# Exponents of the state space decay tables: put together by DMAs instead of by two matmuls in PSUM

## The chip, the cores and the metric

The kernel runs on one core of one Trainium2 chip. The metric is the device time of one execution in microseconds (us), lower is better. Three executions of the kernel before took 2723.22, 2725.10 and 2725.86 us; the median is 2725.1 us. A core has a matrix engine (PE, with its weight loads on a row of their own, PEld), a vector engine (DVE), an activation engine (ACT), GpSimd (POOL), and SyncE (SP), which here only issues DMAs. Each of them works through its own queue in order. Working tiles lie in SBUF; matmuls write to PSUM, which has 8 banks of 128 x 512 numbers.

## The reference, cut to what matters

The model is two blocks of two layers each, for one sequence of 512 positions and width 1024. The change touches one of its mixers, a bidirectional state space layer with 32 heads in 4 groups and chunks of 128 positions. The scan of one direction is, in short:

```python
def step(h, inp):                       # one chunk of 128 positions
    qq, kk, vv, aa = inp                # aa: log decay, <= 0
    cs = jnp.cumsum(aa, axis=1)         # running sum of the log decay
    seg = cs[:, :, None] - cs[:, None, :]
    decay = jnp.exp(jnp.where(mask, seg, -jnp.inf))   # 128 x 128 table of a head and chunk
    qk = jnp.einsum('bjgn,blgn->bjlg', qq, kk)
    y_intra = jnp.einsum('bjlgh,blghp->bjghp', qk[..., None] * decay, vv)
    y_inter = jnp.einsum('bjgn,bghnp->bjghp', qq, h) * jnp.exp(cs)[..., None]
    ...                                 # the state h of the next chunk
y = scan(q, k, v_f, a_f, include the diagonal) + flip(scan(flipped, a_b, without the diagonal))
```

So each head and each direction has a table of exp(running sum at j - running sum at l), cut off by a triangular mask. The kernel adds the tables of the two directions, multiplies by qk once for both, and multiplies the result into v.

## The kernel before, in words

All work is done on transposed activations, 8 tiles of 128 x 512. Matrices of weights come from HBM in pieces of 128 x 1024 (512 KB), each loaded by `wload` (L419 to L429): a DMA on SP's queue into one of 3 buffers `wr`, a rounded copy `wh` on ACT (L427), and the rest `wl` on DVE (L414), each with 3 buffers too. `mm3` (L431 to L435) multiplies one 128 x 128 block of such a piece in three matmuls of 128 x 512, so one piece feeds 24 matmuls.

The state space layer is `ssd`. Its decays are computed early by `dtev`: running sums by matmuls with triangular ones, the natural layout copied out as `c2` twice side by side, transposed (L1141), and split into a rounded half and a rest that lie in the upper and lower 64 partitions of `hl` (L1142, L1143). Then come four groups, each run by `scan(g)`; `weave` (L215) mixes into each scan pieces of the independent large matmuls: `xbc` and `zg` (projections of later groups) and `oproj` (output projection of earlier ones). In `scan(g)`: first states of the chunks (`state`, L1232) and what they contribute (`carry`, three matmuls and an add to `inter` on POOL, L417), and then, head by head, `decay(i)` and, for each pair of heads, `intra(pr)`.

`decay(i)` makes the table of head i for all four chunks, 128 x 512. For each of the two directions it takes a bank of PSUM and makes two matmuls: one with the broadcast selector column of the head, `sel`, on `hl`, which writes the row of running sums into all 128 partitions (L1274), and one with the identity on the mask (L1275), which adds 0 or -1e30. Four exponentials on ACT (L1278), one per chunk, read the bank, add the running sum of the own position as bias, and write SBUF. POOL adds the two directions (L1281), DVE multiplies by qk (L1282). `intra(pr)` multiplies two heads' tables into v in PSUM (L1292) and adds the `inter` tiles by matmuls with the identity (L1296).

SBUF working tiles come from a ring of 78 slots: `T()` takes the slot that was given back longest ago, `rel` gives one back. Nothing checks time there; an instruction that writes a slot waits for the last one that used it. The Tile layer then puts the instructions of the program into one order per engine by readiness, so the order on an engine is not that of the source.

## Time and profile before

The profiled execution took 2723.65 us, with a span of 2721.9 us between the first and the last instruction of the trace, 1.75 us less.

| | before |
|---|---|
| median of 3 executions | 2725.1 us |
| profiled execution, its span | 2723.65 us, 2721.9 us |
| PE busy | 2671.9 us, 98% |
| DVE, ACT, POOL busy | 62%, 45%, 13% |
| mean DMA traffic | 90 GB/s |

Busy time is what a view adds up; matmuls overlap in it, so the mean of one matmul there (some 390 ns) is longer than the time from one start to the next, which is read from the timeline. "Idle before" is the time for which an engine had nothing running before a group's instructions, with the instruction that ended it.

### The profile page before, as it was taken

What the parts mean: (1) busy time and instruction counts of PE and PEld (TensorE: products, weight loads), DVE (VectorE), ACT (ScalarE), POOL (GpSimd) and SP (SyncE); (2) the same over time, 40 slices, a digit from 0 to 9 for tenths busy, and PEclk for the clock granted to TensorE, in tenths of its full rate; (3) what the DMA queues carried; (4) which work ended last, traced back from release to release, by engine and by line L of the source; (5) the groups of instructions that cost most, each with busy time, mean ns of one, the idle gap of its engine ahead of it and who ended that gap; (6) DMA issues with size and microseconds to landing.
All of it is one profiled execution on the core that took longest, in us unless ns stands there. A gap on an engine that the chain in (4) does not pass through costs nothing. (4 is left out here: it accounts for less than half of the span.)

```text
span 2721.9 us, 34509 instructions
## 1 busy us (share of the span) xinstructions
PE 2671.9 (98%) x13136; PEld 2161.2 (79%) x13136; DVE 1674.4 (62%) x3029; ACT 1220.0 (45%) x2136; POOL 345.4 (13%) x416
## 2 busy tenths in 40 slices
PE   9999999999999899999999999999999999999999
PEld 7887888888877677888888877688888888888887
DVE  7765687733898687687762688644343467643442
ACT  5536454422576665554432368633133345432331
POOL 3101300001111211320000245210000100100000
PEclk9999999999999999999999999999999999999999
DMA  4223322243211121323243312223323222323232
GB/s 163 67 90 101 117 93 93 92 123 111 93 56 62 57 68 57 125 82 101 93 127 93 115 43 67 74 69 94 93 93 97 91 79 63 106 89 97 93 99 80
DMA packets 77206, 245.29 MB, mean 90 GB/s; under 512 B 8688, under 2 KB 10096, under 8 KB 77040
## 3 DMA queue, kind: packets, MB, share of 16 engines
q1 hardware_dynamic: 76896, 243.04, 28.3%
q8 instruction: 103, 1.69, 0.3%
q14 instruction: 63, 0.52, 0.1%
q10 hardware_dynamic: 144, 0.05, 0.0%
HBM read 232.57 MB, written 10.49 MB: 89 GB/s over the span
## 5 line engine op out<-in xcount | busy, mean ns | idle before, releaser
L433 PE MATMUL b<-v,wh 128*128 128x512 f32 (+1 forms) x2964 | 1155.5, 390 | 0.3 <-DVE v L1256 0.3
L434 PE MATMUL b<-v,wh 128*128 128x512 f32 (+1 forms) x2964 | 1145.3, 386 | 0.0
L435 PE MATMUL b<-v,wl 128*128 128x512 f32 (+1 forms) x2964 | 1145.0, 387 | 0.2 <-DVE wl L414 0.2
L427 ACT ACTIVATE wh<-wr 128x1024 fp32r<-128x1024 f32 (+3 forms) x401 | 411.4, 1027 | 856.8 <-PE b L434 732.2
L414 DVE TENSOR_TENSOR wl<-wr,wh 128x1024 fp32r<-128x1024 f32 (+3 forms) x401 | 478.0, 1193 | 485.9 <-ACT wh L427 484.0
L433 PEld LDWEIGHTS b<-v,wh 128*128 128x128 f32 x2964 | 557.3, 188 | 123.3 <-issue 3.5
L435 PEld LDWEIGHTS b<-v,wl 128*128 128x128 f32 x2964 | 556.6, 188 | 122.0 <-DVE wl L414 0.9
L434 PEld LDWEIGHTS b<-v,wh 128*128 128x128 f32 x2964 | 557.5, 188 | 120.7 <-issue 2.8
L417 POOL TENSOR_TENSOR v<-v,v 128x256 f32<-128x256 f32 (+1 forms) x146 | 173.5, 1190 | 1535.3 <-ACT v L607 1266.7
L406 ACT ACTIVATE v<-v 128x512 fp32r<-128x512 f32 x172 | 107.9, 630 | 222.8 <-DVE v L1071 101.2
L434 PE MATMUL b<-v,v 128*128 128x256 f32 (+6 forms) x536 | 167.6, 316 | 10.0 <-DVE v L410 8.1
L433 PE MATMUL b<-v,v 128*128 128x256 f32 (+6 forms) x536 | 172.6, 336 | 3.6 <-ACT v L409 2.9
L435 PE MATMUL b<-v,v 128*128 128x256 f32 (+6 forms) x536 | 163.9, 309 | 0.0
L407 DVE TENSOR_TENSOR v<-v,v 128x512 fp32r<-128x512 f32 x172 | 120.7, 706 | 68.8 <-ACT v L406 68.4
L434 PEld LDWEIGHTS b<-v,v 128*128 128x128 f32 (+2 forms) x536 | 101.4, 189 | 24.8 <-DVE v L410 13.3
L433 PEld LDWEIGHTS b<-v,v 128*128 128x128 f32 (+2 forms) x536 | 98.0, 189 | 21.8 <-issue 4.9
L435 PEld LDWEIGHTS b<-v,v 128*128 128x128 f32 (+2 forms) x536 | 101.3, 189 | 5.8 <-issue 0.7
L1060 DVE TENSOR_TENSOR v<-b,v 128x512 f32<-128x512 f32 x88 | 60.4, 690 | 72.4 <-PE b L435 70.6
L409 ACT ACTIVATE v<-v,prm 128x256 fp32r<-128x256 f32 (+1 forms) x112 | 66.4, 598 | 75.1 <-DVE v L265 51.1
L433 PE MATMUL b<-wh,v 128*128 128x512 f32 (+1 forms) x240 | 94.5, 394 | 1.4 <-DVE nv L502 1.1
L434 PE MATMUL b<-wl,v 128*128 128x512 f32 (+1 forms) x240 | 92.4, 385 | 1.0 <-DVE wl L414 1.0
L435 PE MATMUL b<-wh,v 128*128 128x512 f32 (+1 forms) x240 | 92.0, 385 | 0.6 <-DVE v L410 0.6
(372 smaller groups left out, 2706.8 us busy)
## 6 DMA issues: line engine op xcount, KB each, us to landing
wr<-in_w_f SPq DMA_DIRECT2D x128, 512.0 KB, 3.6
wr<-in_w_up SPq DMA_DIRECT2D x88, 512.0 KB, 3.4
wr<-in_w_dn SPq DMA_DIRECT2D x28, 448.0 KB, 3.3
wr<-in_w_xbc SPq DMA_DIRECT2D x24, 512.0 KB, 3.4
wr<-in_w_o SPq DMA_DIRECT2D x20, 512.0 KB, 3.5
wr<-in_w_dn SPq DMA_DIRECT2D x18, 512.0 KB, 3.5
wr<-in_w_z SPq DMA_DIRECT2D x16, 512.0 KB, 3.6
wr<-in_w_co SPq DMA_DIRECT2D x16, 512.0 KB, 3.4
```

Source lines behind the costliest of these rows:

```text
L406: nc.scalar.activation(hi, src, AF.Copy)
L407: nc.vector.tensor_sub(lo, src, hi.bitcast(F32))
L409: nc.scalar.activation(hi, src, AF.Copy, scale=scale)
L414: self.nc.vector.tensor_sub(out, x, y)
L417: self.nc.gpsimd.tensor_add(out, x, y)
L427: nc.scalar.activation(hi, raw, AF.Copy)
L433: mm(ps, lh, rh, start=start, stop=False)
L434: mm(ps, lh, rl, start=False, stop=False)
L435: mm(ps, ll, rh, start=False, stop=stop)
L1060: nc.vector.tensor_mul(h, ps, rb)
```

## The change

The masks leave SBUF: instead of two 128 x 128 tiles in bf16, an input `mdec` in HBM holds both, repeated for the four chunks, as 2 x 128 x 512 numbers. `dtev` copies and transposes the running sums once, not twice side by side, copies them to a tile and writes them to HBM as `csd` (64 rows of 512). For each head and direction a tile of SBUF is then filled in two steps: `masks(i)` loads the mask from HBM by a DMA on SP's queue (256 KB), and `rows(i)` adds the head's row of running sums to all 128 partitions by an accumulating DMA on POOL's queue, whose source is one row of 2 KB of `csd`, broadcast. `masks` is called three heads ahead, `rows` two. The exponentials read that tile and write it in place. The 128 matmuls, their 64 banks and `hl` go.

```diff
-        hl = self.R()
+        csd = self.dp.tile([64, S], F32, name="csd")
...
             for c in range(4):
-                nc.tensor.transpose(b[:, c * P:(c + 1) * P], c2[:, c].rearrange("p a b -> p (a b)"), self.c("id"))
-            nc.scalar.activation(hl, b, AF.Copy)
-            nc.vector.tensor_sub(hl[64:128, :], b[64:128, :], hl[64:128, :].bitcast(F32))
+                nc.tensor.transpose(b[0:64, c * P:(c + 1) * P], c2[:, c], self.c("id"))
+            csT = self.T()
+            nc.scalar.activation(csT[0:64], b[0:64], AF.Copy)
             self.brel(b)
+            nc.sync.dma_start(out=csd, in_=csT[0:64])
+            self.rel(csT)
...
+            def masks(i):
+                if i < 8:
+                    Ex[i] = [self.T(4, P) for _ in range(2)]
+                    for d in range(2):
+                        nc.sync.dma_start(out=Ex[i][d], in_=self.a["mdec"][d])
+
+            def rows(i):
+                if i < 8:
+                    for d in range(2):
+                        r = 32 * d + 8 * g + i
+                        nc.gpsimd.dma_start(out=Ex[i][d].rearrange("p a b -> p (a b)"),
+                                            in_=csd[r:r + 1, :].to_broadcast([P, S]), accum_op=ALU.add)
 
             def decay(i):
+                masks(i + 3)
+                rows(i + 2)
                 h = 8 * g + i
-                t = [None, None]
-                for d, m in ((0, self.mupb), (1, self.mlowb)):
-                    b = self.bank()
+                t = Ex.pop(i)
+                for d in range(2):
                     r = 32 * d + h
-                    nc.tensor.matmul(b, self.sel[:, r:r + 1].to_broadcast([P, P]), hl, start=True, stop=False)
-                    nc.tensor.matmul(b, self.idb, m.unsqueeze(1).to_broadcast([P, 4, P]), start=False, stop=True)
-                    t[d] = self.T(4, P)
                     for c in range(4):
-                        nc.scalar.activation(t[d][:, c], b[:, c * P:(c + 1) * P], AF.Exp,
-                                             bias=nat["sl"][:, c, r:r + 1])
-                    self.brel(b)
+                        nc.scalar.activation(t[d][:, c], t[d][:, c], AF.Exp, bias=nat["sl"][:, c, r:r + 1])
                 nc.gpsimd.tensor_add(t[0], t[0], t[1])
...
             weigh(1, 0)
+            for i in range(3):
+                masks(i)
...
             self.rel(B)
+            for i in range(2):
+                rows(i)
             decay(0)
```

Line numbers of the changed kernel differ from those of before by a few: `mm3` is L430 to L432 there, the mask's DMA L1270, the row's DMA L1277, the exponentials L1288, POOL's add L1289, `intra` L1300 and L1304.

On PE, in the first scan, the matmuls of the first tables stood between the `carry` matmuls (L433 to L435 on `v`) before:

```order
L435 MATMUL b_6959<-v_6884,v_6688 128x512
L1274 MATMUL b_6967<-v_6346,sel 128x512 [waits PE_49]
L1275 LDWEIGHTS idb
L1275 MATMUL b_6967<-mupb,idb 128x512
L1274 MATMUL b_6975<-v_6346,sel 128x512
L1275 LDWEIGHTS idb
L1275 MATMUL b_6975<-mlowb,idb 128x512
L433 MATMUL b_6985<-v_6899,v_6687 128x512 [waits PE_49,Activation_49]
```

In the changed kernel, at the same place, the first matmul of `intra` (L1300) has moved up among the projections (`wh`) and the last `carry`:

```order
L432 MATMUL b_6995<-v_6907,v_6684 128x512
L430 MATMUL b_7007<-v_5954,wh_7009 128x512 [waits PE_49]
L431 MATMUL b_7007<-v_5955,wh_7009 128x512
L430 MATMUL b_7094<-v_5954,wh_7096 128x512
L431 MATMUL b_7094<-v_5955,wh_7096 128x512
L1300 MATMUL b_7145<-v_6759,v_6692 64x128 [waits DMASW1_49,DVE_49]
L430 MATMUL b_7180<-v_5954,wh_7182 128x512 [waits DVE_49,Activation_49]
L431 MATMUL b_7180<-v_5955,wh_7182 128x512
```

What moved: the matmuls of the tables are gone, and nearly all the others keep their order; the first multiplication with a finished table comes earlier, before the last `carry`.

On SP, in the second scan, the weight loads (`wr`) followed each other before:

```order
L426 DMA wr_7777<-in_w_xbc 128x1024 [waits DMAHW7_49,DVE_49]
L426 DMA wr_7834<-in_w_xbc 128x1024 [waits DMAHW0_49,DVE_49]
L426 DMA wr_7928<-in_w_xbc 128x1024 [waits DMAHW1_49,DVE_49,Activation_49]
L426 DMA wr_8016<-in_w_co 128x1024 [waits DMAHW2_49,DVE_49]
L426 DMA wr_8108<-in_w_co 128x1024 [waits DMAHW3_49,DVE_49]
```

In the changed kernel masks stand between them, each with a wait for the last user of its slot (DVE, PE, POOL or ACT):

```order
L423 DMA wr_7996<-in_w_co 128x1024 [waits DMAHW1_49,DVE_49]
L1270 DMA v_7752<-in_mdec 128x512 [waits DVE_49,DMAHW5_49,PE_49,Activation_49]
L1270 DMA v_7725<-in_mdec 128x512 [waits DMAHW6_49,PE_49]
L1270 DMA v_7898<-in_mdec 128x512 [waits DMAHW7_49,PE_49]
L1270 DMA v_7807<-in_mdec 128x512 [waits DMAHW0_49,Pool_49]
L1270 DMA v_7753<-in_mdec 128x512 [waits DMASW2_49,DVE_49]
L1270 DMA v_7808<-in_mdec 128x512 [waits DMAHW2_49]
L1270 DMA v_7724<-in_mdec 128x512 [waits DMAHW3_49,DVE_49]
L423 DMA wr_8072<-in_w_co 128x1024 [waits DMAHW4_49,DVE_49]
L1270 DMA v_7862<-in_mdec 128x512 [waits DMAHW5_49,DVE_49]
L1270 DMA v_7897<-in_mdec 128x512 [waits DMAHW6_49,Pool_49]
L423 DMA wr_8108<-in_w_co 128x1024 [waits DMAHW7_49,DVE_49,Activation_49]
```

What moved: seven masks now stand ahead of one weight load and two more ahead of the next, and one mask of each lot waits for POOL.

On POOL, in the second scan, the two adds of `inter` (L417) were followed by the adds of the tables before:

```order
L417 TENSOR_TENSOR v_7670<-v_7668,v_7653 128x512 [waits DVE_49,Activation_49]
L417 TENSOR_TENSOR v_7726<-v_7724,v_7597 128x512 [waits DVE_49]
L1281 TENSOR_TENSOR v_7731<-v_7731,v_7739 128x512 [waits Activation_49]
L1281 TENSOR_TENSOR v_7761<-v_7761,v_7769 128x512 [waits DMAHW0_49,Activation_49]
L1281 TENSOR_TENSOR v_7818<-v_7818,v_7826 128x512 [waits PE_49,Activation_49]
```

In the changed kernel the rows' DMAs stand around them, each with a wait for its mask (a DMAHW semaphore):

```order
L1277 DMA v_7752<-csd 128x512 [waits DVE_49,DMAHW5_49,PE_49,Activation_49]
L1277 DMA v_7725<-csd 128x512 [waits DMAHW6_49,PE_49]
L414 TENSOR_TENSOR v_7662<-v_7660,v_7645 128x512 [waits DVE_49]
L1277 DMA v_7898<-csd 128x512 [waits DMAHW7_49,PE_49]
L1277 DMA v_7807<-csd 128x512 [waits DMAHW0_49,Pool_49]
L1277 DMA v_7753<-csd 128x512 [waits DMAHW1_49,DVE_49]
L1277 DMA v_7808<-csd 128x512 [waits DMAHW2_49]
L1277 DMA v_7724<-csd 128x512 [waits DMAHW3_49,DVE_49]
L414 TENSOR_TENSOR v_7718<-v_7716,v_7589 128x512 [waits DVE_49]
L1289 TENSOR_TENSOR v_7752<-v_7752,v_7753 128x512 [waits DMASW6_49,DMASW2_49,Activation_49]
```

What moved: seven DMAs now stand ahead of the second `inter` add, and each waits for its mask. The tables of this scan's first three heads are not among these rows: their DMAs and adds stand earlier, in the first scan.

On ACT the 256 exponentials are spread over more places between the SiLU functions of `xbc` and `zg`: its queue holds 45 table loads around them (21 at L1288, 15 at L1163, 9 at L1175) where the kernel before has 31 (13 at L1278, 13 at L1165, 4 at L1177, 1 at L1130).

## Rows read from the trace of the kernel before

**Rows 1.** The page's busy time, share of the span and instructions of each engine.
```profile
PE 2671.9 (98%) x13136; PEld 2161.2 (79%) x13136; DVE 1674.4 (62%) x3029; ACT 1220.0 (45%) x2136; POOL 345.4 (13%) x416
```

**Rows 2.** Windows: stretch, length, busy time by engine, granted clock, DMA share, GB/s.
```profile
690.00:790.00 100.00, 98.55 (x496) 80.69 (x497) 87.20 (x158) 59.12 (x87) 8.38 (x11) 0.98 0.24 80
790.00:1110.00 320.00, 304.02 (x1541) 227.98 (x1540) 244.66 (x337) 205.13 (x434) 72.43 (x50) 0.99 0.19 61
...
796.00:846.00 50.00, 44.96 (x252) 32.58 (x252) 40.13 (x47) 39.32 (x85) 15.94 (x11) 1.00 0.23 74
846.00:870.00 24.00, 23.56 (x108) 19.01 (x109) 22.02 (x42) 11.22 (x15) 0.39 (x1) 1.00 0.10 28
870.00:923.00 53.00, 48.20 (x248) 35.49 (x246) 40.33 (x49) 41.53 (x92) 15.61 (x10) 1.00 0.14 48
...
920.00:930.00 10.00, 3.84 (x13) 2.31 (x14) 6.32 (x6) 7.57 (x17) 3.76 (x3) 0.67 0.11 35
```

**Rows 3.** Waits of PE from 690 to 1120 us: total, times, longest.
```profile
PE b L1292 <- DVE v L1282: 10.4, 4, 4.6
PE b L434 <- DVE v L410: 2.3, 4, 1.2
```

**Rows 4.** Timeline of PE around one head's four matmuls: start, duration, instruction.
```profile
819.34 0.39 PE L435 MATMUL b<-v,wl 128*128 128x512 f32 x1
819.56 0.40 PE L1274 MATMUL b<-v,sel 128*128 128x512 f32 x1
819.80 0.39 PE L1275 MATMUL b<-mupb,idb 128*128 128x512 bf16 x1
819.84 0.58 PE L1274 MATMUL b<-v,sel 128*128 128x512 f32 x1
820.26 0.39 PE L1275 MATMUL b<-mlowb,idb 128*128 128x512 bf16 x1
```

**Rows 5.** Line L1274 and line L1141: duration min/median/max, first and last start.
```profile
L1274 PE MATMUL b<-v,sel x64: 390/578/585, 790.4 to 1106.0; 128*128 128x512 f32 x64
...
L1141 PE MATMUL b<-cst,v x4: 270/272/272, 756.5 to 756.8; 128*128 128x128 f32 x4
```

**Rows 6.** Groups by line on ACT: count, busy us, mean ns, idle before.
```profile
L1278 ACT ACTIVATE v<-b,v 128x128 f32<-128x128 f32 x256 | 69.5, 414 | 4.1 <-PE b L1275 4.0
L427 ACT ACTIVATE wh<-wr 128x1024 fp32r<-128x1024 f32 x47 | 49.5, 1060 | 56.8 <-PE b L434 41.9 <-issue 14.9
L1278 ACT ACT_TABLE_LOAD x13 | 16.7, 1283 | 0.2
...
L1853 ACT ACTIVATE v<-v,gta 128x128 f32<-128x128 f32 x16 | 5.8, 389 | 0.0
```

**Rows 7.** Groups by line on DVE and POOL.
```profile
L414 DVE TENSOR_TENSOR wl<-wr,wh 128x1024 fp32r<-128x1024 f32 x48 | 59.0, 1234 | 15.6 <-ACT wh L427 15.6
L1282 DVE TENSOR_TENSOR v<-v,v 128x512 f32<-128x512 f32 x32 | 29.9, 936 | 27.0 <-POOL v L1281 27.0
...
L1281 POOL TENSOR_TENSOR v<-v,v 128x512 f32<-128x512 f32 x32 | 45.7, 1430 | 96.5 <-ACT v L1278 87.0 <-issue 4.9 <-DVE v L1158 4.5
```

**Rows 8.** DMA issues: KB each, median us from issue to landing.
```profile
wr<-in_w_xbc SPq DMA_DIRECT2D x22, 512.0 KB, 3.4
v<-xs SPq DMA_DIRECT2D x7, 256.0 KB, 2.9
...
outT<-v SPq DMA_DIRECT2D x2, 128.0 KB, 1.7
```

**Rows 9.** Waits of SP's queue from 690 to 1120 us, and its issue, min/median/max ns.
```profile
SPq L426 <- DVE wl L414: 374.8, 44, 34.0
...
L619 SPq DMA_DIRECT2D xf<-v x16: 319/320/432, 318.4 to 1185.2; - x16
```

**Rows 10.** Timeline of PE after its longest wait in the scans.
```profile
923.26 0.61 PE L1292 MATMUL b<-v,v 128*64 128x128 f32 x2 [4.57 <-DVE v L1282]
926.77 1.12 PE L1292 MATMUL b<-v,v 128*64 128x128 f32 x6 [2.90 <-DVE v L1282]
...
928.83 0.63 PE L433 MATMUL b<-v,wh 128*128 128x512 f32 x1
929.26 0.63 PE L434 MATMUL b<-v,wh 128*128 128x512 f32 x1
```

More of the change, by code (lines that the diff above doesn't have):

```diff
@@ L92, in _constants @@
     ramp = ramp.reshape(P, 768)
-    return {"cst": cst, "cs0": cs0.astype(f), "ramp": ramp.astype(f)}
+    mdec = np.stack([np.tile(np.where(p <= c, 0.0, NEG), (1, 4)), np.tile(np.where(p > c, 0.0, NEG), (1, 4))])
+    return {"cst": cst, "cs0": cs0.astype(f), "ramp": ramp.astype(f), "mdec": mdec.astype(f)}
 def _rpb_index():
@@ L324, in __init__ @@
         self.mlab = self.cp.tile([P, P], BF16, name="mlab")
-        self.mupb = self.cp.tile([P, P], BF16, name="mupb")
-        self.mlowb = self.cp.tile([P, P], BF16, name="mlowb")
         self.sel = self.cp.tile([P, 64], F32R, name="sel")
@@ L334, in consts @@
         nc.vector.tensor_copy(self.mlab, self.c("mmla"))
-        nc.vector.tensor_copy(self.mupb, self.c("mup"))
-        nc.vector.tensor_copy(self.mlowb, self.c("mlow"))
         nc.vector.tensor_add(self.sel, self.c("id")[:, 0:64], self.c("id")[:, 64:128])
@@ L1125, in dtev @@
                 nc.tensor.matmul(tot[:, c, :], self.ones, la[:, c, :], start=True, stop=True)
-            c2 = self.T(4, 2, 64)
-            for j in range(2):
-                nc.vector.tensor_copy(c2[:, :, j, :], cs)
+            c2 = self.T(4, 64)
+            nc.vector.tensor_copy(c2, cs)
             nc.scalar.activation(nat["dec"], tot, AF.Exp)
-            nc.scalar.activation(nat["ecs"], c2[:, :, 0, :], AF.Exp)
-            nc.vector.tensor_sub(la, tot, c2[:, :, 0, :])
+            nc.scalar.activation(nat["ecs"], c2, AF.Exp)
+            nc.vector.tensor_sub(la, tot, c2)
             self.brel(b)
@@ L1136, in dtev @@
             nc.scalar.activation(v, v, AF.Ln)
-            nc.vector.tensor_sub(nat["sl"], v.rearrange("p (t h) -> p t h", h=64), c2[:, :, 0, :])
+            nc.vector.tensor_sub(nat["sl"], v.rearrange("p (t h) -> p t h", h=64), c2)
             yield D2
@@ L1264, in carry @@
                     inter[co] = t3
-            W = {}
+            W, Ex = {}, {}
+            def masks(i):
[9 more added lines that the diff above has]
+                                            in_=csd[r:r + 1, :].to_broadcast([P, S]), accum_op=ALU.add)
             def decay(i):
+                masks(i + 3)
+                rows(i + 2)
                 h = 8 * g + i
-                t = [None, None]
-                for d, m in ((0, self.mupb), (1, self.mlowb)):
-                    b = self.bank()
+                t = Ex.pop(i)
+                for d in range(2):
                     r = 32 * d + h
-                    nc.tensor.matmul(b, self.sel[:, r:r + 1].to_broadcast([P, P]), hl, start=True, stop=False)
-                    nc.tensor.matmul(b, self.idb, m.unsqueeze(1).to_broadcast([P, 4, P]), start=False, stop=True)
-                    t[d] = self.T(4, P)
                     for c in range(4):
-                        nc.scalar.activation(t[d][:, c], b[:, c * P:(c + 1) * P], AF.Exp,
-                                             bias=nat["sl"][:, c, r:r + 1])
-                    self.brel(b)
+                        nc.scalar.activation(t[d][:, c], t[d][:, c], AF.Exp, bias=nat["sl"][:, c, r:r + 1])
                 nc.gpsimd.tensor_add(t[0], t[0], t[1])
@@ L1420, in ssd @@
         drain(oproj([3], 2))
-        self.rel(list(nat.values()), hl)
+        self.rel(list(nat.values()))
         st["m"] = m
```

## The prediction

> **What bounds the kernel now.** The page's first part comes first: PE is busy for 98% of the span, DVE for 62%, ACT for 45% [rows 1]. That is an average, so the second view is the windows of the stage that the change touches. The tables are made from 790.4 to 1106.0 us [rows 5]. In 790 to 1110 PE is busy for 304.0 of 320 us, at a granted clock of 0.99, DVE for 244.7, ACT for 205.1 [rows 2]. The third view, who waited for whom, tells what PE's missing time is: 10.4 us, in four places, are the multiplication with a finished table (L1292) waiting for DVE's L1282, the end of the chain exponentials, POOL add, DVE multiply; the next largest is 2.3 us [rows 3]. So PE is the bound here, and a matmul taken out of its queue is worth its distance to the next one, except right in front of these four waits. ACT is second where heads come densely: 39.3 of 50 us from 796 to 846 and 41.5 of 53 from 870 to 923, but 11.2 of 24 between [rows 2].
>
> **The change part by part.** *Matmuls taken out.* Four per head. The start of L435 at 819.34 and those of the four behind it, up to 820.26, are 0.92 us apart, 0.23 us each [rows 4]: 128 x 0.233 = 29.8 us. At the four places where PE then waits anyway the head's 0.93 us may buy nothing, so the term lies between -26.1 and -29.8. I take -29.8 and charge the waits below. The rest (two casts at the start, a copy and a subtraction in `dtev`, transposes of half the columns) is under 1 us and lies beside PE's work; I take 0.
>
> *The exponentials on ACT.* 256 stay. Read from PSUM one takes 414 ns, and the nearest one that reads SBUF 389 ns [rows 6]: 256 x 25 ns = 6.4 us less. The order has 45 table loads in place of 31; 14 x 1.283 us [rows 6] = 18.0 us more. The net, +11.6 us, falls in a stage in which ACT idles for 114.9 of 320 us [rows 2], and the tables of a scan's first heads move out of the dense stretch into the emptier one before it, which works the other way. Both meet in the 10.4 us of waits: these can go (-10.4) or grow by all of ACT's net (+11.6). I take +3, a quarter of the net, since in the dense stretches ACT is busy for nearly four fifths.
>
> *The first table.* It now goes over HBM. From the transposes (L1141, 756.8 us) to the first old table at 790.4 us there are 33.6 us [rows 5]. The new chain is at most 1.06 us to copy (L427's larger copy), 1.7 us to write 128 KB, a row's DMA at 2.9 to 8.7 us (below), a table load of 1.28, eight exponentials of 0.41, POOL's add of 1.43, DVE's multiply of 0.94 [rows 6 to 8]: 12.6 to 18.4 us, and under 25 with four DMAs issued one after the other in front of it. It is hidden: 0. If it were not, the splits for `carry` stand behind these exponentials on ACT, and PE would wait for them directly.
>
> *The masks on SP.* 64 loads of 256 KB, 2.9 us to landing each [rows 8], and SP needs 0.32 us to issue one [rows 9]: 20 us of SP in all. SP mostly waits for free buffers (375 us in 430, for DVE's L414 [rows 9]). What matters is that masks stand in front of weight loads and wait for slots. In the second scan the first lot waits for the `inter` add on POOL, which stands behind DMAs that wait for masks issued a moment before: one trip is 2.9 + a DMA's issue + 1.43, some 5 us, and there are two. A weight piece has three buffers, so when its load is issued two pieces, 2 x 24 x 0.233 = 11.2 us of PE, are still to be used; the load needs 3.4, ACT 1.06, DVE 1.23 [rows 6 to 8], 5.7 us. That leaves 5.5 us for one trip, not for two. Bounds: 0 if SP is never late, and 4 scans x 5 us = +20 if it is late by a whole trip in each. I take +4, one microsecond per scan, because independent matmuls of other pieces stand between.
>
> *The rows on POOL.* 64 DMAs. The trace shows none that POOL issues and none that accumulates. Issue: from 0.32 us (SP's row [rows 9]) to 1.43 us (what POOL takes for an add of 128 x 512 [rows 7]), so 20 to 92 us; POOL is busy for 72.4 of 320 us [rows 2], and either fits. I take 1 us each, nearer to the row of the same engine. Landing: from 2.9 us, a plain load of the same size [rows 8], to three such passes, 8.7 us, if source and destination are each read and then written. I take 2.9 to 5: several are in flight, and rows are called two heads ahead. At that, nothing reaches PE; the upper end is the third rival.
>
> The Trainium skill, page "SBUF — State Buffer", section "Who interferes with whom", speaks against this place: DVE's copies in their two-port mode lock GpSimd out of the port through which it writes DMA descriptors, so a DMA that POOL issues can be held up by DVE, while one that SP issues cannot. No run here shows it yet; by that rule an issue would last up to one DVE instruction longer, and the 1 us above would be 2.
>
> The sum for the profiled execution: 2723.65 - 29.8 + 3 + 4 = 2700.9 us. That execution was 1.45 us below the median of 2725.1, so 2702 is what I expect of the median.
>
> **The rivals.**
>
> *PE gains more.* The waits for L1282 go as well, since tables no longer wait for a bank and a turn on PE, and with them the slow matmuls that follow: after the longest wait, at 923 to 927 us, matmuls start 0.43 us apart, the lower clock of 1.2 GHz (granted 0.67 over 920 to 930 [rows 2, 10]). For it: three heads' tables are finished a scan earlier. Against it: ACT's 14 more table loads, in the very stretches in which ACT was late. 2725.1 - 29.8 - 10.4 - 2 = 2683.
>
> *The waits move to the queues.* Masks in front of weight loads and exponentials in front of weight copies, on in-order queues, make PE wait for weights, which it never does for long now. For it: the masks' waits for POOL, above. Against it: the buffers cover one trip. 2725.1 - 29.8 + 20 + 11.6 = 2727; the half of it is 2711. This is "no change".
>
> *The row transfers become the bound: slower.* All 64 add into 128 rows of 2 KB; if they do not overlap, each must take less than the time that the kernel has per table. From the written sums, 756.8 + 1.06 + 1.7, about 760 us, to the last table at 1106 us [rows 5] that is 346 us, 5.4 us per transfer. Below that point nothing is lost. At 6.0 us the stage takes 384 us in place of 346 and the gain on PE is gone: 2725.1 + 38 = 2763; at 8.7 us, 557 - 346 = 211 us are added, 2936. For it: every transfer reads the same 2 KB 128 times, and the trace shows nothing like it. Against it: plain transfers of this size land in 2.9 us, and the stage moves 61 GB/s at a DMA share of 0.19 [rows 2, 8], so that masks (16.8 MB in 320 us) add 0.16 and rows 0.16 to 0.49: 0.51 to 0.84 in all. The Trainium skill, page "DMA: Bandwidth & Descriptors", section "Rules for kernel authors", says that an accumulating DMA reads its destination and writes it later, which is the three passes; no run here shows it yet.
>
> **How the numbers follow.** The forecast as summed gets 0.46, with a range of its own from 2692 to 2714 (the sum at -33 to -11). More than that on PE gets 0.13. The queues get 0.17, of which 0.09 end within 0.2% of 2725.1 (2719.7 to 2730.5, about what a measurement of this kernel can tell from no change) and 0.08 below it. Slow row transfers get 0.24. So faster is 0.46 + 0.13 + 0.08 = 0.67, same 0.09, slower 0.24. The range from 2687 to 2750 leaves out some 0.06 of the case of more gain and about 0.13 of the slow transfers.
>
> **What would show it.** In the profile after: L1274 and L1275 gone, the stage from the transposes to the last table shorter by 20 to 30 us; the waits of PE for the DVE multiply between 0 and 22 us in total; no waits of PE for L411 (DVE's weight rest there) or for `carry`'s splits above a few us; the rows' DMAs landing in 3 to 5 us, POOL some 64 us longer busy or held by them; the DMA share of 790 to 1110 near 0.5. I would be wrong if the rows land later than 5.4 us one after the other, if ACT's longest waits end with a row's DMA, or if SP's waits end with POOL and PE's with weights.

## The result, and the profile after

The changed kernel takes 2759.5 us (median of 4 runs, 2756.25 to 2764.52) against 2725.5 us before (4 runs): a ratio of 1.0123, 95% interval 1.0112 to 1.0135. It is 34 us slower, where 2702 us, faster, was forecast. The profiled execution has a span of 2756.6 us.

The windows of the changed kernel, to set beside [rows 2] (the columns are the same), show where:

```profile
690.00:790.00 100.00, 98.37 (x497) 79.74 (x497) 84.84 (x153) 63.26 (x112) 22.96 (x25) 1.00 0.49 138
790.00:1110.00 320.00, 271.46 (x1274) 209.30 (x1274) 229.45 (x322) 211.35 (x385) 99.80 (x88) 0.91 0.52 131
1110.00:1140.00 30.00, 18.86 (x102) 15.02 (x103) 13.07 (x17) 13.78 (x37) 13.62 (x13) 0.83 0.57 130
```

In 790 to 1110 us PE was busy for 304.0 us of 320 at a granted clock of 0.99 before; now it is busy for 271.5 at 0.91. The matmuls are gone, and PE stands still more often and runs part of the time at the lower clock. The DMA share of 0.52 is as forecast (near 0.5).

Who waits for whom, PE from 640 to 1200 us (total, times, longest), against [rows 3]:

```profile
PE b L1300 <- DVE v L1290: 16.5, 4, 10.9
PE b L430 <- ACT v L403: 13.4, 4, 6.5
PE b L489 <- POOL v L414: 12.8, 3, 6.1
PE b L430 <- ACT wh L424: 9.3, 1, 9.3
```

Before there was one row of that size, 10.4 us. Now there are four, and three are of work that has nothing to do with the tables: the splits for `carry` (L403), the column sum behind POOL's adds (L414), a weight copy (L424). What these share is an engine that was itself kept waiting. ACT, POOL and SP, 690 to 1140 us:

```profile
ACT v L1288 <- DMA v<-csd: 39.3, 11, 7.8
ACT L1288 <- DMA v<-csd: 15.2, 3, 6.3
POOL v L1277 <- DMA v<-in_mdec: 45.4, 11, 8.0
SPq L1270 <- DVE v L1290: 33.5, 7, 11.1
SPq L1270 <- POOL v L414: 31.2, 6, 13.3
```

ACT's exponentials (L1288) wait 54.5 us for rows, POOL's row transfers (L1277) wait 45 us for masks, and SP's mask loads (L1270) wait for the last readers of the slots that they are to fill. The landings, same window, against [rows 8]:

```profile
v<-in_mdec SPq DMA_DIRECT2D x64, 256.0 KB, 4.3
v<-csd POOLq DMA_DIRECT2D x64, 256.0 KB, 7.1
wr<-in_w_xbc SPq DMA_DIRECT2D x22, 512.0 KB, 3.4
```

Weights land as before. A row takes 7.1 us, POOL's issue included, not the 2.9 to 5 taken. One table, followed through the timelines of SP, POOL, ACT and PE (start, duration, instruction, idle time before it and its releaser):

```profile
1000.15 2.23 SPq L1270 DMA_DIRECT2D v<-in_mdec  x5
...
1003.27 0.86 POOL L1277 DMA_DIRECT2D v<-csd  x1 [15.62 <-DVE v L1238]
...
1003.04 0.63 ACT L403 ACTIVATE v<-v 128x512 fp32r<-128x512 f32 x1 [0.50 <-DVE v L1238]
1010.00 1.28 ACT L1288 ACT_TABLE_LOAD   x1 [6.32 <-DMA v<-csd]
1011.29 0.40 ACT L1288 ACTIVATE v<-v,v 128x128 f32<-128x128 f32 x1
1011.60 0.61 ACT L403 ACTIVATE v<-v 128x512 fp32r<-128x512 f32 x1
...
1012.27 0.79 PE L430 MATMUL b<-v,v 128*128 128x512 f32 x1 [5.29 <-ACT v L403]
1013.00 0.79 PE L431 MATMUL b<-v,v 128*128 128x512 f32 x1
```

The mask goes out at 1000.15, the row 3.1 us later (the view names DVE's L1238 as what released POOL; the mask landed at 1002.73 us, 0.54 us ahead of the row, and in the median of all 64 that distance is 0.52), and ACT, which reaches this exponential in its order after 1003.04, stands 6.32 us until the row is there. Behind it in ACT's order is the split that PE needs: PE stands 5.29 us. Then PE's matmuls last 0.79 us where they lasted 0.39 to 0.40 just before. That is the lower of the clock's two levels (1.2 GHz in place of 2.4): the granted clock was 0.98 in 1000 to 1010 us and 0.68 in the ten us after.

### The profile page after: what moved, and what is told of

The parts are those of the page before. It is cut to its first block, busy times and chain, and to the rows that moved or that the text cites. A ratio compares the mean times of both kernels' runs of the same rounds, so it can differ in the third digit from the quotient of the medians.

```text
span 2756.6 us, 34586 instructions
## 1 busy us (share of the span) xinstructions
PE 2663.5 (97%) x13008; PEld 2160.7 (78%) x13008; DVE 1671.5 (61%) x3025; ACT 1245.7 (45%) x2150; POOL 400.3 (15%) x480
## 3 DMA queue, kind: packets, MB, share of 16 engines
q0 software_dynamic: 9216, 16.78, 3.7%
## 5 line engine op out<-in xcount | busy, mean ns | idle before, releaser
L430 PE MATMUL b<-v,wh 128*128 128x512 f32 (+1 forms) x2964 | 1158.2, 391 | 10.5 <-ACT wh L424 9.3
L432 PE MATMUL b<-v,wl 128*128 128x512 f32 (+1 forms) x2964 | 1146.6, 387 | 3.3 <-DVE wl L411 3.3
L424 ACT ACTIVATE wh<-wr 128x1024 fp32r<-128x1024 f32 (+3 forms) x401 | 411.0, 1026 | 822.9 <-PE b L431 710.0
L430 PEld LDWEIGHTS b<-v,wh 128*128 128x128 f32 x2964 | 560.0, 189 | 133.6 <-ACT wh L424 10.6
L432 PEld LDWEIGHTS b<-v,wl 128*128 128x128 f32 x2964 | 558.6, 188 | 126.8 <-DVE wl L411 4.2
L414 POOL TENSOR_TENSOR v<-v,v 128x256 f32<-128x256 f32 (+1 forms) x146 | 172.2, 1185 | 1335.7 <-ACT v L604 1266.6
L403 ACT ACTIVATE v<-v 128x512 fp32r<-128x512 f32 x172 | 107.5, 629 | 201.1 <-DVE v L1068 101.2
L430 PE MATMUL b<-v,v 128*128 128x256 f32 (+6 forms) x536 | 173.2, 337 | 17.1 <-ACT v L403 13.4
L432 PE MATMUL b<-v,v 128*128 128x256 f32 (+6 forms) x536 | 163.8, 309 | 0.0
L430 PEld LDWEIGHTS b<-v,v 128*128 128x128 f32 (+2 forms) x536 | 97.8, 189 | 37.8 <-ACT v L403 16.2
L1288 ACT ACTIVATE v<-v,v 128x128 f32<-128x128 f32 x256 | 81.9, 391 | 55.4 <-DMA v<-csd 39.3
L432 PEld LDWEIGHTS b<-v,v 128*128 128x128 f32 (+2 forms) x536 | 101.0, 188 | 5.8 <-issue 0.9
L430 PE MATMUL b<-wh,v 128*128 128x512 f32 (+1 forms) x240 | 94.8, 395 | 1.4 <-DVE nv L499 1.1
```

Source lines behind the costliest of these rows:

```text
L403: nc.scalar.activation(hi, src, AF.Copy)
L414: self.nc.gpsimd.tensor_add(out, x, y)
L424: nc.scalar.activation(hi, raw, AF.Copy)
L430: mm(ps, lh, rh, start=start, stop=False)
L432: mm(ps, ll, rh, start=False, stop=stop)
L1288: nc.scalar.activation(t[d][:, c], t[d][:, c], AF.Exp, bias=nat["sl"][:, c, r:r + 1])
```

## The experiments

All times are medians beside runs of the kernel before on the same chip (2725.35 to 2727.77 us); ratios carry the 95% interval. The loss is best placed with the column sum that ends each of the four scans (its first matmul in PE's timeline; after: L489). The changed kernel's rows:

```profile
846.49 1.87 PE L489 MATMUL b<-ones,v 128*128 128x2 f32 x8 [5.02 <-POOL v L414]
957.97 1.44 PE L489 MATMUL b<-ones,v 128*128 128x2 f32 x8 [1.68 <-POOL v L414]
1068.98 1.87 PE L489 MATMUL b<-ones,v 128*128 128x2 f32 x8 [6.11 <-POOL v L414]
1156.99 0.95 PE L489 MATMUL b<-ones,v 128*128 128x2 f32 x8
```

The same matmuls in the other kernels, and the length of scans 2 to 4 from one to the next (us):

| kernel | end of scan 1 | scan 2 | scan 3 | scan 4 | time |
|---|---|---|---|---|---|
| before | 846.4 | 98.6 | 101.3 | 75.7 | 2725.5 |
| after | 846.5 | 111.5 | 111.0 | 88.0 | 2759.5 |
| no transfers | 837.2 | 94.2 | 96.0 | 73.3 | 2702.9 |
| masks alone | 837.2 | 101.0 | 96.1 | 72.5 | 2708.3 |
| plain rows alone | 837.0 | 101.8 | 97.6 | 71.4 | 2708.9 |
| two plain transfers | 840.3 | 109.0 | 104.1 | 80.7 | 2736.6 |
| after, more slots | 846.3 | 96.6 | 104.9 | 77.5 | 2731.1 |
| tables from DRAM, second try | 872.2 | 92.9 | 96.1 | 72.3 | 2736.2 |
| the same, bound behind the sums | 851.8 | 94.8 | 102.5 | 72.6 | 2720.6 |

### Is it the transfers at all, and which?

No transfers:

```diff
-                        nc.sync.dma_start(out=Ex[i][d], in_=self.a["mdec"][d])
...
-                        nc.gpsimd.dma_start(out=Ex[i][d].rearrange("p a b -> p (a b)"),
-                                            in_=csd[r:r + 1, :].to_broadcast([P, S]), accum_op=ALU.add)
...
-  ...activation(t[d][:, c], t[d][:, c], AF.Exp, bias=nat["sl"][:, c, r:r + 1])
+  ...activation(t[d][:, c], self.c(("mup", "mlow")[d]), AF.Exp, bias=nat["dec"][:, c, r:r + 1])
```

> Leaves out both transfers of a table: no mask is loaded and no row is added; the exponentials read a constant mask that stays in SBUF (and take another bias, so that they stay finite) and write the same table tiles. Everything else, the order on each engine, the table's slots and the 21 table loads of ScalarE, is as in the changed kernel. Theory (PE loses its time because a table's two transfers arrive late and in-order queues stand behind them): the waits of ScalarE and GpSimd for DMAs go, 2690 to 2705 us. Rival A (it is the order without the matmuls: more table loads and exponentials bunched on ScalarE, fewer banks' worth of cover): still above 2740 us.

Measured: 2702.9 us, ratio 0.9912 (0.9897 to 0.9927). The order without the matmuls is worth 24 us; rival A falls. The other two leave out one of the transfers: the masks stay (first diff), or the row is written plainly and no mask is loaded (second).

```diff
-                        nc.gpsimd.dma_start(...csd[r:r + 1, :]..., accum_op=ALU.add)
```
```diff
-                        nc.sync.dma_start(out=Ex[i][d], in_=self.a["mdec"][d])
-                                            in_=csd[r:r + 1, :].to_broadcast([P, S]), accum_op=ALU.add)
+                                            in_=csd[r:r + 1, :].to_broadcast([P, S]))
```

> Leaves out the accumulating row transfers alone; masks are still loaded into every table on SP's queue, and the exponentials read them (another bias, so that they stay finite). Theory (the row's landing of about 7 us behind the mask is what comes late): 2690 to 2712 us, near the kernel without transfers. Rival B (the 64 mask loads on SP's queue stand in front of weights and hold them up): 2735 us or more, with SP's waits for freed table slots as now. If both carry a part it lies between, and the distance from the kernel without transfers is the masks' part.

> Leaves out the masks: the row is written into the table by a plain broadcast transfer on the same GpSimd queue, without accumulation, from the same DRAM row, with the same lead. Theory in its first form (adding into the destination is what makes the row slow, 7.1 us in the median): rows land in 3 to 4 us and the time is 2700 to 2715 us. Rival C (the GpSimd queue, or 128 reads of one DRAM row, are slow by themselves): rows still land in 6 us or more, and the time is 2725 us or more. What is left above the kernel without transfers when rows land early is GpSimd's own cost of issuing, 64 x 0.9 us.

Measured: masks alone 2708.3 us (0.9928, 0.9913 to 0.9942), plain rows alone 2708.9 us (0.9932, 0.9915 to 0.9949). A mask or a plain row alone costs 5 to 6 us; a mask and the adding row behind it cost 57. Landings of the two kernels:

```profile
v<-in_mdec SPq DMA_DIRECT2D x64, 256.0 KB, 2.9
```
```profile
v<-csd POOLq DMA_DIRECT2D x64, 256.0 KB, 4.0
```

Neither the masks in front of weights nor POOL's queue nor the one DRAM row costs much by itself: rivals B and C fall. The two traces also show when a table's transfer can start. SP's timeline in the first, POOL's in the second:

```profile
869.89 8.75 SPq L1270 DMA_DIRECT2D v<-in_mdec  x7
...
919.23 1.07 SPq L1270 DMA_DIRECT2D v<-in_mdec  x2
```
```profile
870.11 1.21 POOL L1275 DMA_DIRECT2D v<-csd  x2 [25.39 <-PE b L432]
...
919.52 0.56 POOL L1275 DMA_DIRECT2D v<-csd  x1 [0.85 <-DVE v L1288]
```

These are the 23rd and the 33rd transfer of each kernel. Two queues with different neighbours issue for the same table within 0.3 us of each other, three tables ahead in the one and two in the other; of the 58 behind the first six, 38 go out within 1 us of each other. What sets the time is common to both, and the waits name it: the slot's last reader. Pairing the 64 transfers of each trace, in the order of their queues, with the first exponentials of the 64 tables in ACT's order, the median lead is 6.0 us with masks alone and 6.8 us with plain rows alone. So the lead of two or three tables in the program is 6 to 7 us in time. One transfer of 3 to 4 us fits into it. In the changed kernel the same pairing gives 16.2 us from mask to exponential. That figure holds the two transfers in series (13.3 us in the median from the mask's issue to the row's landing) and the time for which ACT itself was held up, so how late one table is does not follow from it; what it costs ACT is the 54.5 us of waits above.

### Which property of the second transfer?

The row added from a full 128 x 512 source in place of one broadcast row, the adding left out, the mask put in by a POOL copy, and the mask added by POOL to a row that SP loads:

```diff
-  in_=csd[r:r + 1, :].to_broadcast([P, S]), accum_op=ALU.add)
+  in_=self.a["mdec"][d], accum_op=ALU.add)
```
```diff
-  in_=csd[r:r + 1, :].to_broadcast([P, S]), accum_op=ALU.add)
+  in_=csd[r:r + 1, :].to_broadcast([P, S]))
```
```diff
-  nc.sync.dma_start(out=Ex[i][d], in_=self.a["mdec"][d])
+  nc.gpsimd.tensor_copy(Ex[i][d], self.c(("mup", "mlow")[d]).unsqueeze(1).to_broadcast([P, 4, P]))
...
-                masks(i + 3)
+                masks(i + 2)
```
```diff
-  nc.sync.dma_start(out=Ex[i][d], in_=self.a["mdec"][d])
+  nc.sync.dma_start(out=Ex[i][d]..., in_=csd[r:r + 1, :].to_broadcast([P, S]))
...
-  nc.gpsimd.dma_start(..., accum_op=ALU.add)
+  nc.gpsimd.tensor_add(Ex[i][d], Ex[i][d], self.c(("mup", "mlow")[d]).unsqueeze(1).to_broadcast([P, 4, P]))
...
-                rows(i + 2)
+                rows(i + 1)
```

> Leaves out the row: the same accumulating transfers with the same lead, but from a full 128 x 512 source in DRAM in place of one row of 2 KB that all partitions read (and another bias). If accumulation itself is slow: landings of about 7 us and 2750 to 2765 us as before. If it is 128 partitions reading one DRAM row: landings of 4 to 5 us and below 2735 us.

> Leaves out the adding alone: the mask is loaded, and then the row is written over it by the same GpSimd transfer without accumulation (other bias, finite exponentials). Theory (two transfers in series behind a slot that falls free late): mask 3 to 4 us, then row 4 us, 8 to 9 us in series against 11 to 13 with the adding and 4 with one transfer; the time lies between those kernels, 2722 to 2742 us. Rival H (only the adding costs, by its own slowness): 2705 to 2714 us, as with plain rows.

> The row is still added by the accumulating transfer on GpSimd's queue, two tables ahead, but the mask is put into the table by a GpSimd copy from a constant in SBUF just ahead of it, instead of by a DMA: no mask loads, no wait of GpSimd for them. If the wait for masks on GpSimd's in-order queue and the masks' share of the DMA engines were most of the loss, the time comes to 2710 to 2722 us, with rows landing in 4 to 5 us. If the accumulating transfer is slow by itself, rows still land in about 6 to 7 us and ScalarE still waits for them, 2725 to 2745 us.

> Computes the same as the changed kernel by one plain transfer a table and no accumulation: the row is broadcast from DRAM into the table on SP's queue, three tables ahead, where the mask load stood, and GpSimd adds the mask from a constant in SBUF one table ahead of the exponentials (2 x about 1.43 us a table, in place of 2 x 0.9 us of issuing). Theory (the second transfer, the accumulating one, is what costs the changed kernel its gain): rows land in about 3 to 4 us, GpSimd is never waited for by more than a few us, and the time is that of the kernel with plain rows or a little less, 2703 to 2713 us, under the kernel before. Rival E (GpSimd's adds of the mask now lie between row and exponential on an in-order queue, and the table's sum and the square sums stand behind them): 2725 us or more, with ScalarE waiting for GpSimd.

Measured: full source 2761.2 us (one run), landing 6.0 us: rows from one DRAM row land 1.1 us later, but the time is the same, so the broadcast is not it. Two plain transfers in series 2736.6 us (1.0040, 1.0025 to 1.0055), rows landing in 4.7 us, so rival H falls: 28 us of the 51 between one transfer and the changed kernel come with the series alone. The other 23 come with the adding: rows then land in 7.1 in place of 4.7 us, masks in 4.3 in place of 3.7, and POOL takes 0.91 in place of 0.54 us for an issue (medians); these were not told apart, and an adding row with nothing ahead of it in its slot was not run. Mask by POOL copy 2750.3 us (1.0090, 1.0073 to 1.0106), above both ranges: without any mask load the adding row lands in 5.1 us, with copy and issue (means of 1.17 and 1.14 us on POOL) ahead of it. Mask added by POOL 2754.3 us (1.0106, 1.0089 to 1.0123): a plain row of 3.9 us, but two adds of 1.6 us on an in-order POOL between it and ACT; rival E held there, and my hope of a cheap repair fell. Each of the four kernels with two steps in series is slower than the kernel before, by 10 to 35 us.

### Lead, queue or slots?

One table more of lead (with two slots won by packing narrow tables, not shown here), rows of a group's first tables earlier, both; POOL's other adds on DVE:

```diff
-                masks(i + 3)
-                rows(i + 2)
+                masks(i + 4)
+                rows(i + 3)
```
```diff
             for i in range(3):
                 masks(i)
+            for i in range(2):
+                rows(i)
```
```diff
-                    self.pool_add(t3, t, inter[co])
+                    nc.vector.tensor_add(t3, t, inter[co])
...
-                    self.pool_add(sqs[0], sqs[0], sq)
+                    nc.vector.tensor_add(sqs[0], sqs[0], sq)
```

> The same transfers as in the changed kernel, each issued one table earlier (masks four tables ahead, rows three). The two slots that this takes come from packing the four narrow tables of the scan two to a slot. Theory (the chain mask, row, exponential has too little lead): a table takes about 9 us of the scan, so nearly all waits for rows go and the time is 2705 to 2730 us. Rival D (the 16 DMA engines are what is short, their share reaches 1.0 in several stretches): the landings grow by as much as the lead, 2750 to 2765 us. A third outcome, where GpSimd now waits for masks and SP for slots at an earlier place, also leaves the time above 2745 us, but with landings as they are.

> The changed kernel, but the rows of the first two tables of each group are issued right behind the first masks, ahead of the chunk states, and not just ahead of the first exponentials. Theory in the form 'the first tables of a group have no lead' (the longest waits of ScalarE for a row, 5 to 8 us, come once or twice a group): 2725 to 2745 us. If the loss is spread over all tables, or if GpSimd now stands waiting for masks with the sums of carried states behind it: no gain, 2752 to 2765 us.

> Both of these: masks four tables ahead and rows three (with the narrow tables packed to make room, as in the kernel with the longer lead, 2742 us), and the first three rows of a group issued ahead of the chunk states. If lead is all that the accumulating rows lack: 2710 to 2728 us. If the in-order queue of GpSimd (waits for masks with its adds behind) or the slots set it, it stays at 2738 to 2750 us.

> The changed kernel with all its transfers, but the sums of carried states and of squares in the scan are made by VectorE, so that nothing of them stands behind a row's issue on GpSimd's queue. TensorE waited 12.8 us for those adds in the changed kernel. If what stands behind the waiting issue on GpSimd is how the loss reaches TensorE: 2730 to 2745 us. If it reaches TensorE through ScalarE (exponentials that wait for rows, with splits and weight copies behind them): no change, 2752 to 2765 us, and ScalarE's waits for rows stay near 55 us.

Measured: lead 2741.6 us (1.0053, 1.0038 to 1.0068), 18 us back and 12 short of what I expected; early rows 2759.8 us (1.0117), nothing; both 2741.7 us (1.0051); adds on DVE 2763.5 us (1.0135), nothing, though PE's 12.8 us of waits for those adds are gone. Landings stay at 7.2 us with more lead, so rival D is not borne out either. More lead in the program is mostly not more lead in time: by the pairing above a row's issue is 10.2 us ahead of its exponential in place of 9.4. How much of the 18 us is the packing's was not tested.

More free slots, on the changed kernel and, as control, on the kernel before:

```diff
+        self.rel(X[1])
+        X = (X[0], X[0])
...
                 Y[g, pr] = self.split(y2, self.p("cng")[:, 4 * g + pr:4 * g + pr + 1])
+                self.rel(Y[g, pr][1])
+                Y[g, pr] = (Y[g, pr][0], Y[g, pr][0])
```

> The changed kernel with more free slots: the low halves of the stage's input and of its finished outputs are computed as before but given back at once, and the high halves stand in for them in the matmuls (same instructions, other values), so that 8 slots more are free in the first scan and up to 20 more in the last. Theory (a table's slot falls free only 4 to 10 us ahead of its exponentials, whatever the lead in the program, so that a mask and a row, 11 to 13 us in series, end late): masks are now issued 8 us and more earlier, exponentials find their rows landed, 2705 to 2728 us. Rival G (the lead is not set by slots but by SP standing in front of weight loads, or it is traffic): masks go out when they did, 2745 to 2765 us.

> Control for the kernel with more free slots: the same edit on the kernel before, with its matmuls. It loads nothing ahead into slots and TensorE hardly waits for slots in it, so 2716 to 2728 us. If it gained 15 us or more, the gain of the other kernel would not speak for the theory.

> The changed kernel with more free slots (2731 us; same instructions, other values), and the sums of carried states and of squares in the scan on VectorE, so that nothing of them stands behind a row's issue. With the slots GpSimd waited 128 us for masks in the scans and TensorE 11.7 us for its adds. If what is left of the loss there is GpSimd's in-order queue: 2708 to 2722 us. If it is the two transfers in series themselves, or the order: 2726 to 2738 us, as in the changed kernel, where the same move changed nothing.

Measured: 2731.1 us (1.0019, 1.0010 to 1.0028), the control 2719.6 us (0.9977, 0.9967 to 0.9987). Slots bring 28 us to the changed kernel and 7 to the kernel before, so some 21 us of the loss are the slots'. ACT's waits for rows, 690 to 1140 us, are less than half of the changed kernel's 54.5:

```profile
ACT v L1290 <- DMA v<-csd: 18.6, 9, 4.1
ACT L1290 <- DMA v<-csd: 6.0, 1, 6.0
```

I had expected up to 2728; the direction holds, the size falls short. The longer lead that I expected does not show in the median either: the pairing gives 14.7 us from mask to exponential, not more than the 16.2 above. With the adds on DVE as well it is 2731.4 us (1.0024), with PE's 11.7 us of waits for them gone: POOL's adds are not what is left. What remains with more slots (masks 3.9 and rows 5.7 us in series, SP's masks behind weight loads that wait 172 us for buffers) was not taken apart further.

### Is it the traffic? Tables made a scan ahead

Tables in DRAM: masks copied there early, rows added there one scan ahead, one plain load each. First all four scans; then the first scan by matmuls in PSUM; then the rows fed in lots; last, each pair of adding transfers bound behind POOL's sum of the same table. The first, second, third and last edit:

```diff
+            nc.sync.dma_start(out=self.tab[r], in_=self.a["mdec"][r // 32])
...
+                    nc.gpsimd.dma_start(out=self.tab[r], in_=csd[r:r + 1, :].to_broadcast([P, S]), accum_op=ALU.add)
...
-                        nc.sync.dma_start(out=Ex[i][d], in_=self.a["mdec"][d])
+                        nc.sync.dma_start(out=Ex[i][d]..., in_=self.tab[32 * d + 8 * g + i])
...
-                rows(i + 2)
+                fill_row(g + 1, i)
```
```diff
+                t = Ex.pop(i) if g else [None, None]
...
+                    if g:
+                        for c in range(4):
+                            nc.scalar.activation(t[d][:, c], t[d][:, c], AF.Exp, bias=nat["sl"][:, c, r:r + 1])
+                        continue
                     b = self.bank()
                     nc.tensor.matmul(b, self.sel[:, r:r + 1].to_broadcast([P, P]), hl, start=True, stop=False)
```
```diff
+                t = self.T()
+                nc.gpsimd.tensor_copy(t[0:64], csT[0:64])
+                nc.sync.dma_start(out=csg[g, j], in_=t[0:64])
...
+                if i % 2 == 0:
+                    fill_rows(g + 1, i // 2 - 1)
+                    feed(g + 1, i // 2)
```

```diff
+                    f = nc.gpsimd.dma_start(out=self.tab[r], in_=csd[r:r + 1, :].to_broadcast([P, S]), accum_op=ALU.add)
+                    self.tc.add_manual_dep(f.ins, after.ins.name, NOSYNC)
...
-                nc.gpsimd.tensor_add(t[0], t[0], t[1])
+                ad = nc.gpsimd.tensor_add(t[0], t[0], t[1])
+                fill_row(g + 1, i, ad)
```

> Computes the same as the changed kernel and moves more: 64 tables in DRAM are filled with the mask early in the program, one copy of 256 KB behind each of the first 64 weight loads on SP's queue; a group's rows are added there by the same accumulating transfers on GpSimd's queue, a whole group ahead of their use (those of the first group as soon as the running sums are written); and each table comes into SBUF by one plain load of 256 KB on SP's queue where the mask load stood. Theory (the loss is the accumulating transfer's place between a slot and the exponentials, on in-order queues, not its traffic): loads land in about 3 us, ScalarE waits no more than with masks alone, and the time is 2705 to 2716 us. Rival F (traffic: 128 more transfers of 256 KB and GpSimd's 64 issues cost wherever they stand): 2735 us or more, with the DMA share of the scans above 0.5 as in the changed kernel.

> Computes what the reference computes. Tables of the last three scans are made in DRAM (mask copied there from the 25th weight load on, the row added there one scan ahead) and come to SBUF by one plain load of 256 KB, three tables ahead; the first scan makes its tables by the two matmuls in PSUM, as the kernel before, since nothing can be ahead of it. Theory (one transfer in series costs little, wherever the other traffic runs): the kernel without transfers, 2703 us, + 7.5 us for 32 matmuls left in the first scan + 5 to 7 us for the loads' wait = 2714 to 2719 us, under the kernel before. Rival F (traffic at a DMA share above 0.5 costs by itself): 2730 us or more.

> Computes what the reference computes: tables made in DRAM a scan ahead and loaded by one plain transfer, first scan in PSUM, as in the run of 2736 us, but the rows of the next scan are fed to GpSimd in four lots spread over a scan (each lot waits for a small copy into a slot of that scan and its way to DRAM), so that its queue is not full of accumulating transfers when the first scan's table sums come. In the run before TensorE stood still 24.7 us at 823 us for that alone, at GpSimd's 48 transfers 1.27 us apart from 764 to 830 us. Theory (one transfer in series costs little, traffic beside it costs little): 2736 - 25 = 2708 to 2717 us, under the kernel before. Rival F (traffic): 2725 us or more, with waits spread over all scans.

> Computes what the reference computes. As the run of 2736 us (tables made in DRAM a scan ahead, one plain load each, first scan by matmuls in PSUM), but the two accumulating transfers for a table of the next scan are bound behind the GpSimd sum of the same table of this scan, so that its queue holds at most two at a time, and nothing is copied or fed for it. In the run of 2736 us the three later scans took 93, 96 and 72 us from one column sum to the next (kernel without transfers 94, 96, 73; changed kernel 111, 111, 88), and the first one alone lost 26 us, with 48 transfers in GpSimd's queue. Theory (one transfer in series with a late slot costs little, traffic beside it costs little): first scan as in the kernel before, later scans as without transfers, 1122 - 15 = 1107 us at the last column sum and 2707 to 2715 us in all, under the kernel before. Rival F (the accumulating traffic itself slows the scans, and the 72 to 96 us came only because it had run early): later scans of 100 us and more, 2722 us or more.

Measured: 2759.9 us (1.0116), 2736.2 us (1.0040, 1.0027 to 1.0053), 2731.3 us (1.0018, 1.0009 to 1.0027), 2720.6 us (0.9982, 0.9973 to 0.9992). The first three missed what I expected by 44, 17 and 14 us (in the first, scan 1 ends at 889.8 us, 53 us later than without transfers; in the third, scan 3 takes 107.3 us, with a wait of 8.75 us of its column sum for POOL), and the second shows why. PE's timeline and POOL's there:

```profile
798.35 0.40 PE L441 MATMUL b<-v,wh 128*128 128x512 f32 x1
823.41 0.79 PE L442 MATMUL b<-v,wl 128*128 128x512 f32 x1 [24.67 <-DVE wl L417]
```
```profile
812.14 0.81 POOL L1110 DMA_DIRECT2D tab<-csd  x1 [0.52 <-DMA tab<-csd]
...
819.97 1.53 POOL L1311 TENSOR_TENSOR v<-v,v 128x512 f32<-128x512 f32 x1
```

The 48 adding transfers were ready at once, and the scheduler put 39 of them ahead of the first table's sum on POOL. Most then waited for an earlier one (issues some 1.27 us apart), the sum (L1311) came at 819.97 us, DVE stood 24.9 us for it and PE 24.67 for DVE. Scans 2 to 4 of the same run took 92.9, 96.1 and 72.3 us, no more than without any transfer: one load behind a late slot costs nothing there. Of the adding traffic these scans say nothing, because its last transfer had landed at 848.5 us, before they began. The last version runs it beside them. Windows of scans 2 to 4 of the second version, and of scans 2 and 3 of the last:

```profile
872.00:1133.00 261.00, 249.02 (x1235) 195.95 (x1236) 203.76 (x290) 178.95 (x340) 57.64 (x40) 0.96 0.34 111
```
```profile
852.00:946.00 94.00, 84.03 (x403) 64.87 (x403) 72.77 (x99) 68.39 (x122) 33.95 (x32) 0.95 0.68 147
946.00:1049.00 103.00, 95.03 (x474) 75.36 (x473) 82.35 (x113) 68.01 (x130) 27.85 (x27) 0.97 0.58 148
```

Scan 2 of the last version takes 94.8 us beside a DMA share of 0.68, as without transfers (94.2), where the changed kernel takes 111.5 beside 0.46: traffic by itself does not cost it, and rival F falls there. Scan 4 is 72.6 us. Scan 3 is 102.5, with one wait of 5.6 us of the column sum for POOL, in which a part of the traffic is not ruled out, and the first scan, still made by matmuls, ends 5.3 us later than before, with five waits of PE of 1.1 to 3.8 us. Against what I expected these two make most of the difference between 2720.6 and 2707 us. The version is the one here that computes everything and is under the kernel before, by 0.18%, about as much as can be told from none; its profiled execution took 2723.4 us, and there the last column sum comes only 0.5 us earlier than before (1121.6 against 1122.0).

## Why the prediction was wrong

The forecast was 2702, the range ended at 2750, and the sign was wrong. Step by step:

- *Matmuls out, -29.8, ACT's net, +3.* The two together are right in size: without transfers 2702.9 against 2726.7 us, -24, where -27 was their sum. The +3 is luck in part, because the net behind it was misread. One exponential from SBUF is shorter, as taken (mean 391 ns against 414), but exponentials overlap, and what ACT pays is the distance between starts: 293 ns in the median from SBUF, 249 from PSUM. Without transfers they keep ACT busy for 80.8 us in place of 69.5, so 11.3 us more where 6.4 less was taken, and with the 18.0 us of table loads the net is near +29 us, not +11.6.
- *First table, 0.* Right: its exponentials start at 769.2 us, ahead of the old 791.7.
- *Masks on SP, +4.* 5.4 us with masks alone.
- *Rows on POOL, "at that, nothing reaches PE": 0.* This is the step that failed, in two parts. The landing was taken as 2.9 to 5 us; it is 7.1. The upper bound of three passes, 8.7, held the median (single rows took up to 12.5), and I chose the lower end by the row of a plain load. The larger part is the sentence that rows are "called two heads ahead": I counted lead in the order of the program. In time a table's slot falls free 6 to 7 us before its exponentials, with three tables of lead as with two, and mask and row need 11.4 us in series (4.3 + 7.1), 13.3 with what lies between them. [Rows 9] had SP waiting for buffers as a habit; I read it as harmless for weights and did not ask what a mask would wait for. Masks alone and plain rows alone cost 5 to 6 us each; in series they cost 34, and with the adding 57. The terms were summed one by one, and that sum leaves out what they cost in series.
- *The rival of slow rows, 2763 us.* Near the number by another mechanism. It let the transfers run one after the other with 5.4 us as the point of decision. They overlap: 64 x 7.1 = 454 us of landings fit into the 360 us between 763 and 1123, and their queue took 22.7% of the 16 DMA engines in 690 to 1140 us. With plain rows over masks landing in 4.7 us, below that point, the kernel is already some 10 us slower than before.
- *The rival of the queues, 2727 us.* It had the right places (waits move to SP, exponentials stand in front of weight copies and splits) and charged one trip for the masks and ACT's net, not the wait for rows.
- *What would show it.* ACT's longest waits do end with a row's DMA, as written for being wrong; 31.2 us of SP's waits end with POOL and 9.3 of PE's with a weight copy.

ACT's exponentials without transfers, 690 to 1140 us, to set beside the first line of [rows 6]:

```profile
L1283 ACT ACTIVATE v<-cst,v 128x128 f32<-128x128 f32 x256 | 80.8, 390 | 9.8 <-PE b L1230 4.5 <-DVE v L1286 2.3 <-POOL v L414 1.2
```

Two rules of the Trainium skill were weighed there. The Trainium skill, page "DMA: Bandwidth & Descriptors", section "Rules for kernel authors", says that an accumulating DMA reads its destination and writes it later. The trace fits that, though it shows no reading as such: the same 16.78 MB went in 9216 packets at 22.7% with adding and in 5120 at 13.2% without, 1.7 times the time. The Trainium skill, page "SBUF — State Buffer", section "Who interferes with whom", says that DVE's two-port copies hold up GpSimd's writing of descriptors. The runs neither show nor exclude it: an adding issue took 858 to 2557 ns, 29 of 64 of them above 1 us, but a plain issue of POOL took 538 to 709 ns in all 64, beside the same work of DVE.

## What to carry to other kernels

A transfer issued "n steps ahead" is ahead in time only if its buffer is free by then: read, in the trace, when the buffer's last reader ends, and compare that with the sum of all steps in series behind it. Two cheap transfers in series on in-order queues can cost far more than each alone, here 34 us against 5 to 6, because the engines that wait hold up work that has nothing to do with them. Where a value must be put together by a slow transfer, do that in a place of its own and bring it in by one load, which here undid the loss and won next to nothing beyond it; and bind such transfers to a point in the order, since a ready transfer may be put in front of everything.

## What the runs showed that I had not expected

- An adding transfer of 256 KB lands in 5.1 us with no mask loads beside it, 7.1 with them, and in DRAM in 7.9 to 13.9 us; the same row written plainly takes 4.0.
- POOL takes 0.54 us to issue a plain transfer (median, 538 ns) and 0.91 an adding one, and with 48 in its queue issues were some 1.27 us apart.
- Exponentials of 128 x 128 that read SBUF start 293 ns apart, those that read PSUM 249, although one of the former is the shorter (391 against 414 ns).
- PE's wait of 5.29 us that ends at 1012.27 us is followed by matmuls of 0.79 and 0.63 us in place of 0.40, at a granted clock of 0.68 in 1010 to 1020 us. That is part of such a wait's price.
